# First weight sum of gate/up tiles 1 to 4 by two DMAs, and rewritten issue orders, in a fused SSD + latent-attention + SwiGLU layer

## The chip, the cores and the metric

The kernel runs on one core of one Trainium2 chip. The metric is device time in microseconds of one execution; several executions are timed and their median is given. The engines of the core are TensorE (PE; the loading of its stationary operand is listed apart, as PEld), VectorE (DVE), ScalarE (ACT), GpSimd (POOL) and SyncE (SP), which here only issues DMAs. Each engine carries out its own list of instructions in order; between engines semaphores order the work.

## The reference

One layer of a hybrid encoder for 512 prompt and 64 sample tokens (576 columns in all), width 1024, followed by a final norm. Everything is float32.

```
h = rmsnorm(x);  z, xbc, dt, cq, ckv, kr = split(h @ w_in)
y_ssd = rmsnorm(ssd_scan(silu(conv(xbc)), dt, ...) * silu(z))       # chunked state space heads
o     = mla_attend(q(cq), keys(ckv, kr)) @ w_uv                     # latent attention, block-causal
x = x + concat(y_ssd, o) @ w_out
hf = rmsnorm(x)
x = x + (silu(hf @ w_gate) * (hf @ w_up)) @ w_down                  # D_FF = 2816
y = rmsnorm(x)
```

The change touches the weights of `hf @ w_gate` and `hf @ w_up`.

## The kernel before

All activations lie transposed, features on the 128 partitions and tokens along the free axis; 576 tokens are two halves of 288. Float32 accuracy is reached by three products of fp32r operands: every weight and activation is split into a high part (a cast on ScalarE, L127) and a low part (a subtraction on VectorE, L128).

**Stages.** In-projection (0 to about 35 us), convolution and state sums, the SSD scan, attention, out-projection (to about 255 us), gate/up and down (to about 600 us), final norm. In the feed-forward part D_FF is cut into 22 tiles of 128 columns; tile f has one step for gate and up (`gu_steps`, tile 0 in `gu_first`), and after every four tiles a down step (`down_steps`), part of whose results is added into `x2` by accumulating DMAs from GpSimd's queue (L1047).

**Seven products in place of eight.** Gate and up of one tile and the two halves of the tokens form a 2x2 block product, calculated by the Strassen/Winograd scheme: `block_product` (L894) multiplies one of A11, A12, S4, A22, S1, S2, S3 with one of seven sums of activation blocks. The weight sums S1 to S4 are made on the chip, in `block_weights`:

- `r2` and `r1`, 128 x 1024 floats each (512 KB), are loaded on SP's queue (L847, L848). One half of each holds one block of the 2x2.
- L850: left half of `s1` = left of `r2` + right of `r2`. This is S1.
- L851: left half of `s2` = left of `r2` - left of `r1` (S3).
- L852: right half of `s1` = S1 - left of `r1` (S2).
- L853: right half of `s2` = right of `r1` - S2 (S4).
- Then A22, A11/A12, S1/S2 and S3/S4 are split: casts on ScalarE (L855, L127), subtractions on VectorE (L861, L128).

In the trace `gu` stands for all of `r2`, `r1`, `s1`, `s2` (named gu{f}_0, _1, _2, _3 in this order), `wh_gu_S`, `wl_gu_S`, `wh_gu_A`, `wl_gu_A` and `gu_a` for their split forms. The down weights (`db`) go through the same function.

**Slots.** The buffers of the four raw tensors come from a pool of 8 slots of 4 KB per partition, and a table (`PLACES`) says which buffer gets which slot. Around the change: slot 0 holds an out-projection weight, then gu1_2, gu3_2 and a down weight; slot 2 an out-projection weight, gu2_2, gu4_2, gu5_2; slot 4 gu1_0, gu2_0, gu4_1; slot 1 gu1_1, gu2_1, gu4_0, gu5_0; slots 3 and 5 hold out-projection weights and then gu3_0 and gu3_1; slot 6 gu2_3 and gu4_3; slot 7 gu1_3 and gu3_3. A load into a slot waits until the last reader of the buffer before it is done.

**Order.** The engines don't issue in the order of the program. At the end of the file `issue_in_order` (L1274) takes, for each of the five engines, a list in `ISSUE` that names the engine's instructions by their number of creation, and ties each to its predecessor in that list. So the place of an instruction in a list fixes which instructions of its engine stand ahead of it; it starts when these have been issued and its operands are there. The steps of each stage are created in the order of `ORDER_CONV`, `ORDER_SSD`, `ORDER_ATT` and `ORDER_FFN`.

Of the kernel before, what the change touches and what calls it, by code (L numbers as in the profile page):

```python
# [37 lines left out]
BLOCKS = tuple(range(0, LAST - 1, 4))  # L38
SEEDED = (4, 5, 6, 7)
# [17 lines left out]
def hybrid_layer_kernel(ctx: ExitStack, tc: tile.TileContext, a, o):  # L57
# [783 lines left out]
    def block_weights(src1, src2, name, blocks):  # L841

        n = len(gu_dma)
        sums = dve
# [5 lines left out]
        sums.tensor_tensor(l(s1), l(r2), r(r2), ALU.add)  # L850
# [423 lines left out]
def issue_in_order(tc, nc):  # L1274
# [45 lines left out]
602-612 637 641-644 638-640 657-659 665-688 660 689-736 661-662 737-760 771-794 663-664 645-652 763-766 653-656  # L1320
795-818 767-770 761-762 819-826 859-861 833-836 862-864 827-832 865-866 837-839 867 880-883 840 868-870 841 845-852
871-873 853-856 874-879 842-843 904-906 857-858 884-887 907-909 844 888 910-912 892-903 889-891 913-915 925-934
916-921 935 939-940 922-924 936-938 949-957 964-965 941 966 945-948 967-969 942-944 970-971 958-963 972-974 976-979
975 987-988 980 984-985 1003 991-993 981-983 986 1015 1004-1006 989 994-995 1016-1021 996 1007-1014 1022-1026
1029-1034 997 1043-1045 990 1000-1002 998-999 1046-1054 1035-1042 1027-1028 1059-1060 1055 1075-1092 1056-1058
1093-1104 1121-1123 1065-1067 1124 1061-1062 1071-1072 1063-1064 1130-1132 1068-1070 1125-1129 1073 1133-1156
1105-1108 1074 1229-1237 1119-1120 1238 1241 1239-1240 1242-1252 1157 1111-1114 1109-1110 1253-1264 1158 1176
1265-1276 1115-1118 1159-1161 1177-1179 1162-1175 1277-1285 1289-1290 1180-1183 1188-1189 1184-1187 1205-1206
1190-1192 1227 1193-1198 1291-1297 1199-1201 1228 1202-1204 1286-1288 1215-1220 1207-1214 1221 1318 1222-1224 1298
1225-1226 1299-1306 1319 1307 1320 1308-1317 1321-1322 1330-1332 1323 1342-1343 1348-1351 1344-1345 1352-1354 1346  # L1330
1355 1347 1333 1324-1329 1334-1341 1356-1363 1368 1364-1366 1369-1370 1367 1371-1393 1404 1394-1396 1405-1406
1397-1403 1407-1415 1428 1416-1427 1429-1433 1440-1441 1434-1435 1442 1436-1439 1572 1443-1447 1452 1448 1453-1456
1449 1457-1458 1450 1459-1460 1451 1461-1462 1587 1578 1584 1463 1581 1573 1464-1478 1579 1479-1486 1575 1488 1487
1489 1585 1490-1497 1500 1498 1501-1503 1499 1586 1588 1504-1506 1576 1574 1507 1580 1508-1509 1512 1577 1513 1510
1514-1515 1511 1516-1517 1605 1518-1522 1593 1523-1525 1582-1583 1526-1527 1606 1528-1531 1602 1536 1532 1537 1533
1538 1534 1603 1539 1607 1535 1589 1540-1541 1599 1542-1544 1594 1608 1545-1550 1600 1551-1552 1595 1614 1553-1555
1609 1560 1556-1557 1626 1561-1565 1615 1558-1559 1566-1568 1616 1569-1570 1604 1571 1596 1590 1597-1598 1601 1591
1610 1617 1620 1623 1621 1635 1627 1622 1592 1636 1629 1637 1628 1611 1641 1618 1630 1624 1631 1612-1613 1625
1658-1659 1642 1644 1650 1660 1647 1661-1662 1632-1633 1663 1651 1648 1664-1665 1619 1656 1638-1640 1666 1643 1667
1634 1668 1645 1669 1646 1649 1652-1654 1657 1694 1670-1672 1695-1697 1673 1682 1698 1655 1674 1699 1675 1700 1718  # L1340
1683 1719 1676-1677 1701 1678 1684 1702 1679 1685 1703 1680 1704 1686 1681 1720 1687 1721 1688 1722-1723 1689 1724
1690-1691 1706 1692-1693 1725 1707 1726 1705 1727-1728 1708-1709 1730 1710-1711 1729 1712 1731-1732 1713-1717
1733-1734 1778-1779 1735 1780 1754 1736 1755 1742 1756 1743-1744 1781 1737 1782 1745-1746 1766 1747-1749 1767 1783
1750-1752 1738 1768 1753 1757-1758 1769 1739-1740 1759 1741 1770 1784 1760 1785-1786 1771 1787 1761-1762 1802 1788
1803 1772 1789 1763 1773 1804-1805 1774 1806-1813 1764-1765 1775-1776 1838 1777 1839-1841 1862-1864 1842 1865
1843-1846 1866 1790 1867 1814 1847 1791 1848 1868 1792 1849 1869 1793 1870-1872 1794-1795 1873 1815-1818 1874-1875
1819 1796 1820 1797 1876 1798-1799 1877 1800 1878-1880 1850-1851 1881 1801 1821 1882 1822 1883 1823 1884 1852-1853
1826 1885 1827 1824 1828 1825 1829 1854 1830-1831 1855 1832 1856 1886-1887 1833 1857-1860 1888 1834 1889-1890 1861
1891 1835 1892 1836 1893 1837 1894-1900 1910-1913 1901-1903 1922 1946 1923 1904 1914-1915 1905-1907 1947 1924 1948
1916-1917 1934-1937 1925 1918-1919 1949 1920 1938 1926-1927 1939-1940 1921 1950 1928 1908 1929 1909 1951 1930 1952  # L1350
2024 1941 1970 1931 2025 1971 1932-1933 1942-1944 1953 1972 1945 1954-1956 1958-1959 1973 1960 1974-1975 1961 1976
1962-1963 1977 1964 2026 1965-1966 2027-2028 1967 1978 1957 2029 1968-1969 2000 1979 2012 1980-1982 2054 1983
1988-1989 2042 2013 1990 2043 2055 2006 2056 2014-2015 1991 2007 2001 2044 2048 1992-1993 2057 2002 2058-2059 1984
2008-2009 2045 2016 2003-2005 1985-1986 2017 2049 2046-2047 1994 1987 1995 2010 1996 2011 2018 1997 2060-2061 2019
2062 2020-2021 2030 2063 2022 2031 2064 2023 2065-2066 2050 2067-2069 1998 2032 2070 2051-2052 1999 2053 2033
2071-2073 2034 2074-2075 2084-2086 2076 2078 2035 2077 2079 2036 2087 2080-2081 2037 2088 2082 2114 2083 2102 2090
2089 2038 2091 2103 2039-2040 2115 2092 2041 2093 2104 2094 2105 2095 2106 2096 2107 2116-2118 2138 2097-2099 2139
2108 2100 2109 2101 2119 2110 2192 2111-2112 2120 2113 2121 2126 2122 2127 2123 2128-2130 2140 2131 2144 2132 2145
2193 2133 2124 2134 2146-2148 2135 2149-2150 2136 2194 2137 2141 2125 2142 2195-2196 2151 2143 2197 2156 2152-2153
2157-2158 2154 2159 2168 2160-2162 2180 2155 2163 2181 2169 2164-2165 2182 2174 2222 2170-2171 2216 2166 2210 2175  # L1360
2172 2183 2173 2167 2184 2223 2217 2176 2211 2177 2224 2186 2212 2225 2187-2188 2218 2178-2179 2219 2213-2215 2185
2189-2190 2226 2191 2234 2198 2220 2199-2200 2235 2228-2230 2221 2204 2231-2232 2236 2201 2237-2239 2233 2227
2205-2206 2240 2202 2246 2241 2203 2242 2252 2243-2245 2207 2247 2253-2254 2248 2270 2255 2208 2282 2256-2258 2283
2259-2260 2271-2272 2261 2284 2262-2264 2273 2285 2209 2265 2286 2266 2274 2267 2275 2268 2287 2269 2288-2289 2276
2290 2277 2249 2306 2291-2292 2294 2278 2295 2307 2279 2296 2280-2281 2297-2303 2293 2318-2319 2308 2304 2309-2310
2320 2305 2311 2250 2321-2323 2312-2313 2251 2314 2330 2315-2316 2331 2317 2332-2333 2324 2334-2335 2325-2326 2336
2354 2327 2366-2367 2337 2342 2338 2368-2370 2343 2339-2340 2371 2355 2328 2344-2348 2356 2349 2372 2341 2350-2352
2357 2373-2374 2358 2353 2390 2375 2359-2361 2376 2362-2363 2329 2364-2365 2377-2382 2391-2393 2402-2403 2394
2404-2405 2383-2385 2395 2386 2406 2387 2407 2388-2389 2408 2396-2398 2409 2399-2400 2410 2401 2414-2418 2438 2411
2419-2420 2426-2428 2421 2429 2422 2450 2412 2423-2424 2451 2439 2430-2431 2413 2452 2440 2432 2425 2453 2441-2442  # L1370
2433 2443-2444 2434 2445 2435 2446 2436 2447 2437 2454 2528 2474 2448 2529 2455-2457 2530 2449 2531-2532 2475-2476
2462 2477 2533 2458-2459 2463-2464 2478-2479 2465-2466 2480 2558 2467 2481 2468-2471 2482 2472-2473 2483 2516 2559
2484-2485 2460 2486 2461 2487 2492 2517 2493 2560 2518 2546 2504 2494 2488 2519 2552 2495-2497 2553 2505 2520 2547
2506-2507 2521 2548 2498-2499 2549 2489 2500 2510 2501 2508 2502 2550-2551 2561 2490 2509 2554 2503 2511 2491 2555
2512-2513 2562-2563 2514-2515 2570 2522-2523 2571 2524 2556 2525 2564 2526-2527 2557 2534-2535 2565 2572 2566-2569
2540 2582-2584 2573 2541 2574 2542 2585 2575-2576 2536-2539 2588 2577 2589 2586 2578-2579 2590 2543 2580-2581
2591-2592 2606-2609 2544 2610 2594-2595 2545 2593 2587 2596-2597 2611-2613 2598 2618 2599-2601 2619 2614 2602
# [123 lines left out]
685 682 681 688-690 679 692 687 693-700 691 701-704 683 705-719  # L1501
# [111 lines left out]
```

## Time and profile before

| | |
|---|---|
| Median of 3 runs | 640.44 us (639.99 to 640.5) |
| Profiled execution, its own time | 639.58 us |
| Profiled execution, span | 637.5 us |
| Granted TensorE clock | 0.998 |
| Weights of gate/up | 44 loads of 512 KB, one L850 add for each of 22 tiles |
| GpSimd | 111 instructions, none between 192 and 304 us |

The span reaches from the first to the last instruction of the profile; the run's time has 2.1 us more around it. In the rows that follow, a line number belongs to the kernel above, `out<-in` are the names of the program with buffer numbers left out, and `xN` counts instructions. TensorE's matmuls are pipelined: one of 288 columns shows a duration of about 0.29 us, while the next one starts 0.13 us after it, so durations overlap and starts count.

### The profile page before, as it was taken

Reading aid. Unit: us, or ns where it says so; the run is one execution under the profiler, and the core shown is the slowest. Engines: PE = TensorE matmul, PEld = TensorE weight load, DVE = VectorE, ACT = ScalarE, POOL = GpSimd, SP = SyncE. Lnnn points to the kernel's source line nnn. Section 1 sums busy time; section 2 is a strip of 40 time slices with the busy share of each in tenths; the row PEclk is TensorE's granted clock in tenths of the full one; section 3 lists DMA queues with packets and bytes.
Section 4 is the critical chain, followed back from the end, with each engine's and each line's share of the span. In section 5 each row is a group of like instructions: output and inputs, shape, how many; then the busy total and the mean of one; then the engine's idle time right before and its main releaser. Section 6 shows DMA issues by size and latency. Waiting matters only on the chain.

```text
span 637.5 us, 11950 instructions
## 1 busy us (share of the span) xinstructions
PE 626.2 (98%) x4639; PEld 598.0 (94%) x4639; DVE 551.4 (86%) x980; ACT 390.4 (61%) x751; POOL 70.7 (11%) x111
## 2 busy tenths in 40 slices
PE   9999999999999999999999999999999999999994
PEld 9899999985887899999999999999999999999994
DVE  6999996899867599999998997889888998998763
ACT  7655425789766479955656565655565656545463
POOL 1322122001010000000012002100211011100022
PEclk9999999999999999999999999999999999999999
DMA  9522185314131132231187427550765274723004
GB/s 310 207 51 78 35 209 151 114 30 147 72 111 34 62 131 73 93 108 67 36 202 158 128 91 163 141 136 40 189 159 133 67 182 111 181 74 133 1 1 149
DMA packets 31560, 72.66 MB, mean 114 GB/s; under 512 B 3706, under 2 KB 11400, under 8 KB 31248
## 3 DMA queue, kind: packets, MB, share of 16 engines
q1 hardware_dynamic: 25360, 60.77, 29.8%
q0 software_dynamic: 5424, 10.57, 9.3%
q8 instruction: 36, 0.59, 0.4%
q10 hardware_dynamic: 720, 0.57, 0.3%
q14 instruction: 20, 0.16, 0.1%
HBM read 58.03 MB, written 3.30 MB: 96 GB/s over the span
## 4 chain that ended last, share of the span: by engine, by line
PE 48%; issue 1%; DVE 1%; ACT 1%; POOL 1%; POOLq 0%; DVEq 0%
PE ps_x L894 17%; PE ps_dx L1034 9%; PE ps_z L894 9%; PE ps_dz L1034 5%; PE ps_y L894 4%; PE ps_dy L1034 2%; PE ps_l L1104 2%; POOL x L1157 0%; DVE x L1145 0%; DVE sq_last L1194 0%; DVE ss L1192 0%; POOL ss L1238 0%; POOLq L1600 0%; ACT sq L1233 0%; ACT x L1149 0%
## 5 line engine op out<-in xcount | busy, mean ns | idle before, releaser
L894 PE MATMUL ps_x<-xop,wh_gu_S 128*128 128x288 f32 x504 | 126.2, 295 | 0.0
L894 PEld LDWEIGHTS ps_x<-xop,wh_gu_S 128*128 128x128 f32 x504 | 88.2, 188 | 0.7 <-ACT u L963 0.2
L894 PE MATMUL ps_x<-xop,wl_gu_S 128*128 128x288 f32 x252 | 73.2, 295 | 0.0
L894 PE MATMUL ps_z<-xop,gu_a 128*128 128x288 f32 x252 | 61.7, 295 | 0.0
L127 ACT CAST wh_gu_S<-gu 128x1024 fp32r<-128x1024 f32 x44 | 46.2, 1053 | 14.8 <-PE ps_y L894 4.2
L128 DVE TENSOR_TENSOR wl_gu_S<-gu,wh_gu_S 128x1024 fp32r<-128x1024 f32 x44 | 52.8, 1217 | 0.8 <-ACT wh_gu_S L127 0.5
L894 PEld LDWEIGHTS ps_x<-xop,wl_gu_S 128*128 128x128 f32 x252 | 47.1, 188 | 0.0
L1047 POOL DMA_DIRECT2D x<-db x16 | 14.9, 930 | 277.9 <-ACT db L1040 247.8
L143 PE MATMUL ps_in<-xs,wh_in 128*128 128x288 f32 x256 | 45.5, 298 | 0.0
L894 PE MATMUL ps_y<-xop,wh_gu_A 128*128 128x288 f32 x168 | 44.9, 295 | 0.0
L894 PEld LDWEIGHTS ps_z<-xop,gu_a 128*128 128x128 f32 x252 | 43.5, 188 | 0.0
L894 PE MATMUL ps_z<-xop,wh_gu_S 128*128 128x288 f32 x168 | 43.4, 295 | 0.0
L894 PE MATMUL ps_x<-xop,wh_gu_A 128*128 128x288 f32 x168 | 42.7, 295 | 0.0
L143 PEld LDWEIGHTS ps_in<-xs,wh_in 128*128 128x128 f32 x256 | 37.8, 189 | 0.2
L127 ACT CAST wh_gu_A<-gu 128x1024 fp32r<-128x1024 f32 x22 | 23.1, 1051 | 23.0 <-PE ps_x L894 16.1
L894 PEld LDWEIGHTS ps_y<-xop,wh_gu_A 128*128 128x128 f32 x168 | 30.1, 188 | 0.1
L894 PEld LDWEIGHTS ps_z<-xop,wh_gu_S 128*128 128x128 f32 x168 | 29.7, 188 | 0.0
L128 DVE TENSOR_TENSOR wl_gu_A<-gu,wh_gu_A 128x1024 fp32r<-128x1024 f32 x22 | 26.8, 1217 | 3.3 <-ACT wh_gu_A L127 1.8
L894 PEld LDWEIGHTS ps_x<-xop,wh_gu_A 128*128 128x128 f32 x168 | 29.5, 188 | 0.0
L465 PE MATMUL ps_o<-cat_y,wh_out 128*128 128x288 f32 x128 | 29.0, 312 | 0.0
L143 PE MATMUL ps_in<-xs,wl_in 128*128 128x288 f32 x128 | 27.5, 296 | 0.0
L465 PE MATMUL ps_o<-cat_o,wh_out 128*128 128x288 f32 x128 | 27.3, 297 | 0.0
(594 smaller groups left out, 2002.8 us busy)
## 6 DMA issues: line engine op xcount, KB each, us to landing
gu<-in_w_gu SPq DMA_DIRECT2D x44, 512.0 KB, 4.8
db<-in_w_down SPq DMA_DIRECT2D x16, 512.0 KB, 4.5
x<-db POOLq DMA_DIRECT2D x16, 288.0 KB, 6.5
x<-dc POOLq DMA_DIRECT2D x16, 288.0 KB, 4.1
wr_in<-in_w_in SPq DMA_DIRECT2D x8, 512.0 KB, 6.2
wr_out<-in_w_out SPq DMA_DIRECT2D x8, 512.0 KB, 3.3
cumb<-cumD SPq DMA_DIRECT2D x5, 512.0 KB, 5.0
x<-in_xT SPq DMA_DIRECT2D x2, 1152.0 KB, 6.6
```

The costliest lines, as they stand in the source:

```text
L127: act.copy(hi, raw)
L128: dve.tensor_tensor(lo, raw, hi.bitcast(F32), ALU.subtract)
L143: pe.matmul(ps[:m, hf, :n], w, x[:, hf * n : (hf + 1) * n], start=start and k == 0 and i == 0, stop=stop and k == last and i == 2,)
L465: pe.matmul(ps[:, :n], w, x[:, cols], start=not onto and k == 0 and i == 0, stop=onto or (k == len(terms) - 1 and i == 2), skip_group_chec ...
L894: pe.matmul(ps, p, q, start=not onto and first and kp == kps[0] and j == 0, stop=onto or (last and kp == kps[-1] and j == 2), skip_group_c ...
L1034: pe.matmul(ps, l, r, start=not onto and k == 0 and j == 0, stop=onto or (k == n - 1 and j == 2), skip_group_check=onto,)
L1047: pool.dma_start(x2[t], v, accum_op=ALU.add)
L1104: pe.matmul(ps, w, x[:, cols], start=first and k == 0 and i == 0, stop=last and k == len(terms) - 1 and i == 2,)
```

## The change

For the four tiles named, S1 is no longer an add on VectorE. A second load brings the left half of the same source once more, straight into the left half of `s1` (128 x 512 floats, 256 KB, SP's queue); then GpSimd's queue issues an accumulating DMA that adds the right half of the source to it (256 KB). Everything that follows from S1 stays as it was. The second DMA waits for the first, both wait for the slot of `s1`, and L852 and the split of S1 wait for the second.

The lists of `ISSUE` are rewritten: the first place that differs is 630 of TensorE's (about 94 us in the trace of before), 156 of VectorE's (about 96 us), 78 of ScalarE's (about 93 us), 74 of GpSimd's and 40 of SP's. Up to there nothing differs. TensorE and ScalarE keep the number of their instructions; VectorE's list is four shorter, SP's and GpSimd's four longer each. `PLACES` is unchanged.

```
+SUMS_BY_DMA = ('gu1', 'gu2', 'gu3', 'gu4')
...
         sp.dma_start(shaped(r2), src2)
         gu_dma.append(sp.dma_start(shaped(r1), src1).ins)
         l, r = ((lambda z, i=i: (blocks if z is r1 or z is r2 else halves_of)(z)[i]) for i in range(2))
-        sums.tensor_tensor(l(s1), l(r2), r(r2), ALU.add)
+        if name in SUMS_BY_DMA:
+            sp.dma_start(s1[:, :512], src2[:, :512])
+            pool.dma_start(s1[:, :512], src2[:, 512:], accum_op=ALU.add)
+        else:
+            sums.tensor_tensor(l(s1), l(r2), r(r2), ALU.add)
         sums.tensor_tensor(l(s2), l(r2), l(r1), ALU.subtract)
         sums.tensor_tensor(r(s1), l(s1), l(r1), ALU.subtract)
         sums.tensor_tensor(r(s2), r(r1), r(s1), ALU.subtract)
...
     "POOL": """
-0-3 7 18 28 4 8 5 9 6 10 26-27 11 29 12-17 20-22 19 23-25 31 30 32-42 53 55 57 59 54 56 58 60 43-52 61-73 75 74 76-77
-79 78 80-85 87 86 88-89 91 90 92-93 95 94 96-111
+0-3 7 18 28 4 8 5 9 6 10 26-27 11 29 12-17 20-22 19 23-25 31 30 32-42 53 55 57 59 54 56 58 60 43-52 61-77 79 78 80-81
+83 82 84-89 91 90 92-93 95 94 96-97 99 98 100-115
 """,
     "SP": """
-11-14 16 15 18 17 19-20 22 21 25 24 39 23 37 26 40 33 38 41-43 34 44 32 45 81 46-48 57 64 79 59 58 56 62 61 65 63 60
-83 70 74 67 69 68 71 78 80 88 73 75 72 66 89 77 76 82 86 90-92 87 93 100 103 101-102 104-105 109-118 120 119 122-123
...
+11-14 16 15 18 17 19-20 22 21 25 24 39 23 37 26 40 33 38 41-43 34 44 32 45 81 46-48 57 64 79 59 58 56 62 61 60 65 63
+83 70 68-69 74 67 78 71 80 75 66 73 72 88 77 76 89 82 91 86 90 87 92-93 100 103 101-102 104-105 109-111 114-115 112
+116 113 117-118 120 119 121-122 124 123 126 125 128 127 130 129 131-132 134 133 135-140 142 141 144 143 145-146 148
...
```

Read out, SP's list around these tiles is, before and after ("S1" is the new load):

| before | after |
|---|---|
| gu1_0, gu1_1 | gu1_0, gu1_1 |
| gu2_0, gu2_1 | S1 of gu1, S1 of gu2 |
| gu3_0, gu3_1 | gu3_0, gu2_0, gu3_1, gu2_1 |
| gu4_0, gu4_1 | S1 of gu3, gu4_0, S1 of gu4, gu4_1 |
| db0_0_0, db0_0_1 | db0_0_0, db0_0_1 |

GpSimd's four new DMAs stand behind the last of its attention work (about 178 us) and ahead of the first accumulating DMA of the down step (about 319 us). Places of some instructions in VectorE's list, counted from 0: L852 of tile 1 was 414 and is 418; the subtraction of tile 1's S1/S2 (L128) was 445 and is 441; L852 of tile 2 was 430 and is 445; L852 of tile 3 was 468 and is 460; L852 of tile 4 was 483 and is 475. In TensorE's list changes between a matmul of plain fp32 operands and one of fp32r operands number 108 before and 192 after.

More of the change, by code (lines that the diff above doesn't have):

```diff
@@ L1324 @@
[L1324 to L1333, printed above, removed]
@@ new lines @@
+1749-1751 1737 1752 1784-1785 1767 1756 1786 1768 1753 1787 1769 1757 1738 1770 1739 1802 1758 1740 1771 1741
+1759-1760 1772 1788 1803-1805 1789 1806-1807 1761 1808-1813 1762 1773-1774 1763-1764 1775 1765 1776 1838-1839 1777
+1862 1840 1863-1864 1841-1842 1790 1865 1843-1846 1866 1847-1848 1867 1849 1791 1868 1792 1814 1869-1872 1874 1793
+1875 1794 1873 1815 1795-1796 1816 1797 1817-1818 1798 1850 1799-1800 1819-1820 1876 1801 1821 1877-1878 1851
+1879-1882 1822 1883 1852 1823 1826 1853-1854 1824 1884 1827-1828 1885 1825 1829-1830 1855-1857 1831 1886 1832
@@ new lines @@
+4190 4162 4206 4169 4191 4163 4192 4226 4170 4227 4238 4164 4171 4165 4193 4198 4172 4199-4200 4173 4201 4174 4239
+4175-4177 4194 4184 4240 4202 4207 4228-4229 4241 4230 4208-4209 4231 4195 4185 4242 4210 4243 4186 4232 4211-4212
+4262 4213 4263 4233-4234 4223 4214 4244 4217 4203 4235 4264 4236 4245 4204 4218 4220 4215-4216 4224 4265 4225 4221
+4266 4219 4267 4246 4237 4268 4250-4252 4247 4253 4274-4275 4254 4276-4277 4248 4222 4278 4269-4272 4249 4279 4273
+4255-4259 4280 4260-4261 4281-4391
@@ L1477 @@
+890 918 912 866 914 920-921 898 924 891 923 925 933 892 922 928 927 926 935 934 936 930 929 931-932 937-938 942 940
+939 943 947 941 945 944 950 946 948-949 951-975
 """,
@@ new lines @@
+563 566 564 569 568 567 571 570 561 572 565 577 574 578 575 573 580 582 576 579 589 586 581 588 587 583 592 590 597
+584-585 591 594 602-603 595 599 596 600 605 601 598 604 606 611 593 609 608 610 612-613 630 614 607 619 624 616 625
+615 617 621 618 622 626 623 620 627-628 633 631 636-637 629 634-635 632 640 638-639 643 645 644 648 646 651 654 649
+641 647 656 655 650 657 659 658 663 660-661 642 664-666 652 674 667 675 669 653 662 670 668 676-677 671 673 672 678
+680 686 684 682 688 690 692-699 687 700 689 701 681 683 679 685 702-704 691 705-719
```

331 lines of the change are left out of this document (166 added, 165 removed).

## The prediction

> **What bounds the kernel now.** First the page's totals and the chain of work that ended last:
>
> ```profile
> span 637.5 us, 11950 instructions
> PE 626.2 (98%) x4639; PEld 598.0 (94%) x4639; DVE 551.4 (86%) x980; ACT 390.4 (61%) x751; POOL 70.7 (11%) x111
> PE 48%; issue 1%; DVE 1%; ACT 1%; POOL 1%; POOLq 0%; DVEq 0%
> ```
>
> TensorE sets the end: it is busy for all but 11.3 us of the span, and the named part of the chain is nearly all TensorE. An edit pays only where it takes a hole out of TensorE's stream, and costs only where it makes one. So I read next the busy time by stretches, around the edited sums and where the order lists begin to differ (columns: busy us of PE, PEld, DVE, ACT, POOL with instruction counts, granted clock, DMA share, GB/s).
>
> ```profile
> 80.00:224.00 144.00, 142.74 (x1041) 121.76 (x1040) 113.18 (x248) 93.51 (x244) 14.40 (x25) 1.00 0.34 105
> 144.00:160.00 16.00, 14.75 (x76) 9.54 (x76) 15.77 (x41) 15.23 (x44) 1.96 (x4) 1.00 0.45 146
> 224.00:336.00 112.00, 111.90 (x831) 110.37 (x830) 110.88 (x185) 79.04 (x134) 3.38 (x4) 1.00 0.33 101
> 240.00:256.00 16.00, 16.00 (x122) 15.92 (x121) 15.79 (x30) 15.43 (x32) 0.00 (x0) 1.00 0.20 67
> 256.00:272.00 16.00, 16.00 (x117) 15.54 (x116) 15.97 (x31) 14.23 (x25) 0.00 (x0) 1.00 0.32 104
> 288.00:304.00 16.00, 16.00 (x122) 15.92 (x122) 15.26 (x25) 8.99 (x14) 0.00 (x0) 1.00 0.20 67
> ```
>
> VectorE is full from 224 to 336 us (110.88 of 112), yet TensorE has no hole there (111.90 of 112). VectorE sits just under the limit and not on it. At 144 to 160 us TensorE does run dry for 1.25 us, and that stage lies inside the rewritten part of the order lists. In the gate/up stage a better order could only shorten the pitch of the matmuls: 831 starts at 16/122 = 0.131 us are 109.0 us of the 112, so 3.0 us at most, and some of that is slower kinds of matmul (the norm sums among them).
>
> **What is removed.** Four adds at L850, of tiles 1 to 4. Their group, and three neighbours from VectorE's timeline (start, duration, line):
>
> ```profile
> L850 DVE TENSOR_TENSOR gu<-gu x22: 678/681/694, 222.8 to 573.2; 128x512 f32<-128x512 f32 x22
> 286.49 0.68 DVE L853 TENSOR_TENSOR gu<-gu,gu 128x512 f32<-128x512 f32 x1
> 287.09 0.68 DVE L850 TENSOR_TENSOR db<-db 128x512 f32<-128x512 f32 x1
> 287.69 0.45 DVE L971 TENSOR_TENSOR g<-ps_y,R 128x288 f32<-128x288 f32 x1
> ```
>
> One add lasts 0.68 us, but the next instruction starts 0.60 us after it (287.09 to 287.69), so four give back 4 x 0.60 = 2.4 us of VectorE. Does TensorE see it? The first of this time comes free before 262 us, and there ScalarE stands in the way:
>
> ```profile
> 260.57 1.05 ACT L127 CAST wh_gu_S<-gu 128x1024 fp32r<-128x1024 f32 x1
> ```
> ```profile
> 239.52 0.68 DVE L850 TENSOR_TENSOR gu<-gu 128x512 f32<-128x512 f32 x1
> 249.04 0.46 DVE L820 TENSOR_TENSOR xv<-xv 128x288 f32<-128x288 f32 x1
> 262.09 1.21 DVE L128 TENSOR_TENSOR wl_gu_S<-gu,wh_gu_S 128x1024 fp32r<-128x1024 f32 x1
> 264.32 0.44 DVE L914 TENSOR_TENSOR u<-u,ps_p 128x288 f32<-128x288 f32 x1
> ```
>
> The subtraction for tile 1's S1/S2 (262.09) needs the cast that ends at 260.57 + 1.05 = 261.62. By count of the new list, VectorE would reach it at 262.09 - 2.4 = 259.7: two adds are gone (1.2), and two operations of tile 2 ahead of it have moved behind it (1.2). ScalarE's list up to that cast ends as before and ScalarE is 15.43 of 16 busy at 240 to 256 us, so I don't expect an earlier cast. VectorE then idles about 1.9 us and the gain there is spent. The value for the removal is -0.4 us, between 0 (TensorE has no hole to fill) and -2.4 (every freed microsecond reaches it).
>
> **What is added.** Per tile a 256 KB load on SP's queue and a 256 KB accumulating one on GpSimd's. No row shows these; the nearest are the two accumulating groups' statistics (288 KB; issue ns, then issue to landing), and a plain 256 KB load:
>
> ```profile
> L1047 POOL DMA_DIRECT2D x<-db x16: 862/862/1205, 318.8 to 543.1; - x16
> DMA to landing us min/median/max: 3.4/4.8/8.2
> wr_uqr<-in_w_uqr SPq DMA_DIRECT2D x1, 256.0 KB, 2.6
> ```
>
> So a sum is ready 2.6 + 0.86 + 4.8 = 8.3 us after its slot is free, between 6.9 and 11.7. GpSimd has nothing else to do between 192 and 304 us, so its waits delay nobody. [...]
>
> Tile 1: the slot is free by 239.52 (the old add writes it then), so the sum is there at 247.8 (246.4 to 251.2). Its first reader, L852, is at place 418 of the new list: all that before had done by 249.04 except the add, L852 and L853, so 249.04 - 1.8 = 247.2. Stall 0.6 (0 to 4.0); the idle 1.9 us at S1/S2 covers the middle value. Tile 3's slot is free once tile 1's S1/S2 is subtracted, 261.6 + 1.1 = 262.7, plus 8.3 = 271.0 (269.6 to 274.4). Its reader stands, in operations of 0.37, 0.60 and 1.14 us pace, some 10 us behind that subtraction, at about 272.9: no stall at the middle, 1.5 at the upper end. Tiles 2 and 4 have likewise about 9.6 us between freeing and reading. I take 0 for all four, 0 to 4.0 as bounds.
>
> **What is moved past a queue.** SP's queue issues in order, and the new list puts tile 2's loads behind tile 3's first. SP's rows of before, and a burst of four 512 KB loads to price the new one:
>
> ```profile
> 243.62 0.33 SPq L847 DMA_DIRECT2D gu<-in_w_gu  x1
> 246.33 0.33 SPq L848 DMA_DIRECT2D gu<-in_w_gu  x1
> 255.41 0.33 SPq L847 DMA_DIRECT2D gu<-in_w_gu  x1
> 255.84 0.38 SPq L848 DMA_DIRECT2D gu<-in_w_gu  x1
> ```
> ```profile
> L134 SPq DMA_DIRECT2D wr_dl<-in_w_dlast x4: 328/376/426, 577.3 to 579.2; - x4
> DMA to landing us min/median/max: 3.5/5.2/7.4
> ```
>
> Tile 3's first load waits at 255.41 for a slot that an out-projection weight holds. Tile 2's pair, at 243.62 and 246.33 in before, now follows it: about 255.8 and 256.6, the second being the last of four. It lands 3.5 to 7.4 us later, 260.1 to 264.0; I take 264.0, as it is the last of its burst like the 7.4 row. VectorE's first reader of it, L852 of tile 2, moved from 253.44 to place 445: 264.32 less four operations of 0.60 (two adds, and L851 and L852 of this tile) is 261.9, or 261.62 + 1.14 + 3 x 0.37 = 263.9 with the ScalarE wait above. Stall 0.1 (0 to 2.1). Measured against before's pace, VectorE must start it by 264.32 - 1.2 = 263.1 to lose nothing; it is 0.9 us late, and the two adds still to vanish (tiles 3, 4) give 1.2 back. ScalarE's cast of tile 2's A11 stands at about 266 us, behind the landing. Cost on TensorE: 0 (0 to 0.9).
>
> **The rewritten order.** From about 93 us on all lists differ, though the work is the same. TensorE changes between fp32 and fp32r matmuls 192 times instead of 108, counted in the lists. Its timeline prices a change:
>
> ```profile
> 165.25 0.29 PE L465 MATMUL ps_q<-cqn,wl_pair 128*128 128x288 f32 x1
> 165.39 0.27 PE L702 MATMUL ptp<-ident,pr 128*128 128x128 f32 x1
> 165.41 0.62 PE L465 MATMUL ps_k<-ckv,wh_pair 128*128 128x416 f32 x2
> 165.88 0.35 PE L465 MATMUL ps_k<-ckv,wl_pair 128*128 128x416 f32 x1
> 166.06 0.59 PE L680 MATMUL sc<-ks,qs 100*128 100x256 f32 x2
> 166.50 0.71 PE L702 MATMUL ptp<-ident,pr 128*128 128x128 f32 x5
> 166.96 0.62 PE L465 MATMUL ps_k<-ckv,wh_pair 128*128 128x416 f32 x2
> 167.42 0.35 PE L465 MATMUL ps_k<-ckv,wl_pair 128*128 128x416 f32 x1
> ```
>
> A 416-column fp32r matmul takes 166.06 - 165.88 = 0.18 to 0.19. One transposition alone: 165.88 - 165.25 = 0.63, less 0.13 and 2 x 0.19, is 0.12. Five in a row: 167.42 - 166.50 = 0.92, less 0.38, over five is 0.108. So a pair of changes costs about 0.012 us, and 42 more pairs 0.5 us (0 to 0.5 for this kind; the kinds that use half the columns may be dearer). I take +0.5. The order's effect on waits I can't see ahead: TensorE's idle 1.26 us between 80 and 224 us (144.00 less 142.74) could vanish or double, -1.3 to +1.3, value 0.
>
> **Sum.** 639.58 (profiled run: span 637.5 and 2.1 around it) - 0.4 + 0 + 0 + 0.5 + 0 = 639.7. The median of the runs stands 0.86 us above the profiled run, so the forecast is 640.5, written 640.6: no change, within the 0.2% (1.28 us) that a measurement of this kernel can tell.
>
> **Rivals.**
> *Freed VectorE time reaches TensorE, and the new order closes the attention stage's hole.* For it: VectorE 110.88 of 112, so every list in that stage hangs on it, and 117 starts in 256 to 272 us against 122 nearby (5 x 0.131 = 0.7 us). Against it: TensorE's 111.90 of 112, and ScalarE's cast. Price: 0.7 + half of the 1.26 us hole + half of the other adds' 1.2 = 1.9 us, so 638.5.
>
> *Tile 2's second load decides (the other side).* One mechanism: SP's queue at 255.4 us. If it lands after 263.1, VectorE, full until 336 us, passes the delay on: to the release of the PSUM banks behind it (L914), to R2, to the low halves that TensorE's tile 1 and 2 products read. For it: four 512 KB loads in a burst, and a moved issue 10 us later. At 264.0 it costs 0.9; with tile 3's sum at its upper end as well delayed by the same shift, and tile 4's behind it, up to 0.9 + 1.5 + 1.5 = 3.9. Middle 2.4: 642.9. Against it: TensorE's products of tile 2 begin only at 266.7 us, and other tiles' products can run between. [...]
>
> *The new order starves TensorE in the attention stage.* For it: 144 to 160 us, where VectorE is 15.77 and ScalarE 15.23 of 16: transpositions, their copies and the products that read them are placed closer there in the new lists. Against it: elsewhere in 80 to 224 us VectorE is 113.18 of 144. Price: the 1.26 us hole once more, and half again, 1.9 us: with the switches 642.4.
>
> *The sums aren't taken from the path because the path never was there* (the change does what it says and it is worth nothing) is the forecast itself.
>
> **How the numbers follow.** Forecast 0.32 (own range 639.2 to 641.8), first rival 0.30, second 0.24, third 0.14. Faster than 639.16: 0.30 and 0.03 of the forecast = 0.33. Slower than 641.72: 0.38 and 0.04 = 0.42. Same: 0.25. The range: downwards the first rival with all of the hole and the full 0.7 and 1.2, 640.5 - 3.2 = 637.3; upwards tile 2's case with 3.9, 644.4.
>
> **What would show it.** Right: L850 x18 in its group; the TensorE window 256 to 272 us still 16.00 with about 117 starts; VectorE idle before the S1/S2 subtraction, released by ScalarE, near 262 us; tile 2's loads on SP at about 255.8 and 256.6; the waits of L852 on a DMA under 1 us in all. Wrong, to the fast side: 80 to 224 us shorter by over 1 us, or over 119 starts in 256 to 272. Wrong, to the slow side: L852 waiting for a DMA by over 2 us and a named TensorE wait on VectorE behind it, or new waits on L702 and L727 between 140 and 224 us.

## The result, and the profile after

| | before | after |
|---|---|---|
| Median of 6 runs each | 640.47 us (639.78 to 640.84) | 647.7 us (644.76 to 649.72) |
| Profiled execution: its time, span, granted clock | 639.58, 637.5, 0.998 | 644.76, 643.1, 0.993 |

The changed kernel is slower: 1.0111 times the time before, 95% interval 1.0077 to 1.0145, or 7.2 us. The forecast was 640.6, the range ended at 644.4. Its six runs lie in two groups, 644.76, 645.48 and 645.87 us (clock 0.990 to 0.993) and 649.54, 649.64 and 649.72 us (0.985 to 0.988), and the profiled one is of the first group, so its trace explains 5.2 us (644.76 less 639.58). A second trace of the same kernel, further down, shows what a longer run has more.

The page after: totals, and the chain of work that ended last.

```profile
span 643.1 us, 11977 instructions
PE 628.0 (98%) x4639; PEld 600.1 (93%) x4639; DVE 553.2 (86%) x976; ACT 390.7 (61%) x751; POOL 74.2 (12%) x115
PE 74%; DVE 11%; DMA 6%; issue 5%; ACT 3%; POOL 1%; POOLq 0%; SPq 0%; DVEq 0%; ACTq 0%
```

VectorE, ScalarE and DMA now stand in a chain whose named part had been TensorE's almost alone. Busy time by stretches, columns as in the prediction:

```profile
80.00:224.00 144.00, 140.84 (x1024) 120.09 (x1024) 114.95 (x246) 93.65 (x243) 13.60 (x25) 1.00 0.33 100
96.00:112.00 16.00, 15.31 (x119) 15.09 (x118) 11.05 (x17) 8.31 (x23) 2.59 (x3) 1.00 0.49 141
144.00:160.00 16.00, 14.14 (x73) 9.65 (x72) 15.32 (x39) 14.06 (x40) 1.96 (x4) 1.00 0.25 87
224.00:336.00 112.00, 112.00 (x839) 111.30 (x838) 109.81 (x181) 77.61 (x134) 7.01 (x8) 1.00 0.43 125
336.00:600.00 264.00, 262.96 (x1979) 262.03 (x1978) 234.15 (x373) 154.32 (x262) 24.22 (x28) 1.00 0.48 125
```

And before, the two stretches that the prediction did not show:

```profile
96.00:112.00 16.00, 16.00 (x124) 16.00 (x124) 10.82 (x18) 9.36 (x26) 3.24 (x4) 1.00 0.51 148
336.00:600.00 264.00, 264.00 (x1992) 263.74 (x1991) 235.88 (x374) 153.70 (x260) 24.37 (x29) 1.00 0.48 125
```

Read the starts of TensorE, at 0.131 us each; in microseconds this is an estimate, since not all matmuls are of one size. From 80 to 224 us 17 are missing (1024 for 1041, 2.2 us), of which 96 to 112 us, the state sums, has 5. The stretch with the edited sums has 8 more than before (839 for 831, a gain of 1.0 us), and the feed-forward behind it 13 fewer (1.7 us). So the stage of the edit gained, and the loss is where the order changed and the edit is not. Whether the edit or its stage's order gained, this trace doesn't tell; a pair of kernels further down does. From 600 us on, two matmuls of the final part give fixed points:

```profile
624.46 0.28 PE L1104 MATMUL ps_l<-pr,wl_dl 128*128 128x256 f32 x1
627.19 1.83 PE L1251 MATMUL ps_warm_last<-ones 128*128 128x128 f32 x14
629.03 1.16 PE L1257 MATMUL ps_r<-Rp,ident 128*128 128x128 f32 x8
```
```profile
626.78 0.28 PE L1109 MATMUL ps_l<-pr,wl_dl 128*128 128x256 f32 x1
630.74 3.15 PE L1256 MATMUL ps_warm_last<-ones 128*128 128x128 f32 x14
633.68 1.40 PE L1262 MATMUL ps_r<-Rp,ident 128*128 128x128 f32 x8
```

First fence before, second after (line numbers are 5 higher there: L857 is the old L852). The last product of the down step (`ps_l`) starts 626.78 - 624.46 = 2.32 us late; from it to the last broadcast of the norm (`ps_r`) it is 6.90 us where it was 4.57, another 2.33; and from `ps_r` to the end of the span 9.42 for 8.47, 0.95. That is the whole 5.6 us of span. The fourteen matmuls on ones into `ps_warm_last` are the same work in both: 1.83 us at a granted clock of 1.00 and 3.15 us at a mean of 0.54.

**Who waits in the state sums.** ScalarE, VectorE and GpSimd around 95 us, before:

```profile
93.17 0.69 ACT L410 ACTIVATE cth<-cacc 128x579 f32<-128x579 f32 x1 [5.67 <-DVE cacc L408]
94.79 0.21 DVE L413 SCALAR_TENSOR_TENSOR bc<-cth,cacc 128x64 f32<-128x64 f32 x1
96.07 0.68 POOL L523 TENSOR_SCALAR_AFFINE_SELECT cumb<-cumb 64x512 f32<-64x512 f32 x1
```

After:

```profile
94.76 0.67 ACT L411 ACTIVATE cth<-cacc 128x579 f32<-128x579 f32 x1
95.46 0.23 DVE L414 SCALAR_TENSOR_TENSOR bc<-cth,cacc 128x64 f32<-128x64 f32 x1 [0.89 <-ACT cth L411]
95.97 2.08 DVE L413 SCALAR_TENSOR_TENSOR bc<-cth,cacc 128x512 f32<-128x512 f32 x1
95.77 1.72 POOL L524 TENSOR_SCALAR_AFFINE_SELECT cumb<-cumb 64x512 f32<-64x512 f32 x2
```

The new ScalarE list puts other work ahead of the last tanh of the convolution, so it comes 1.6 us later (94.76 for 93.17). The 512-column part of VectorE's product of that tanh (`bc`) then falls together with GpSimd's selects and lasts 2.08 us. Before, the 64-column part was over at 95.00, ahead of the select. TensorE loses 0.69 us at 96 to 112 us (15.31 of 16.00) by this. More of the idle time lies in the attention stage: from 136 to 168 us TensorE's holes are 0.12, 0.20, 1.66 and 0.40 us by stretches of 8 us, 2.38 us in all, where before had 1.25. The waits named there are for ScalarE and VectorE, ahead of the scores (0.44 and 0.48 us) and of the transpositions (0.74, which were 0.92 and 0.21 before).

### The profile page after: what moved, and what is told of

It reads as the page before. It is cut to its first block, busy times and chain, and to the rows that moved or that the text cites. A ratio compares the mean times of both kernels' runs of the same rounds, so it can differ in the third digit from the quotient of the medians.

```text
span 643.1 us, 11977 instructions
## 1 busy us (share of the span) xinstructions
PE 628.0 (98%) x4639; PEld 600.1 (93%) x4639; DVE 553.2 (86%) x976; ACT 390.7 (61%) x751; POOL 74.2 (12%) x115
## 4 chain that ended last, share of the span: by engine, by line
PE 74%; DVE 11%; DMA 6%; issue 5%; ACT 3%; POOL 1%; POOLq 0%; SPq 0%; DVEq 0%; ACTq 0%
PE ps_x L899 16%; PE ps_z L899 8%; PE ps_o L466 8%; PE ps_in L144 7%; PE ps_dx L1039 6%; PE ps_y L899 4%; PE ps_dz L1039 3%; PE ps_z L466 3%; PE ps_first L144 2%; DMA x<-db 2%; PE ps_l L1109 2%; PE sc L681 2%; PE ps_p L899 2%; PE ps_dy L1039 2%; PE pv L728 1%
## 5 line engine op out<-in xcount | busy, mean ns | idle before, releaser
L899 PE MATMUL ps_x<-xop,wh_gu_S 128*128 128x288 f32 x504 | 123.8, 295 | 0.3
L128 ACT CAST wh_gu_S<-gu 128x1024 fp32r<-128x1024 f32 x44 | 46.1, 1052 | 10.8 <-PE ps_x L899 4.3
L899 PE MATMUL ps_y<-xop,wh_gu_A 128*128 128x288 f32 x168 | 46.2, 295 | 0.0
L899 PE MATMUL ps_x<-xop,wh_gu_A 128*128 128x288 f32 x168 | 44.0, 295 | 0.0
L128 ACT CAST wh_gu_A<-gu 128x1024 fp32r<-128x1024 f32 x22 | 23.1, 1051 | 23.0 <-PE ps_x L899 11.6
L466 PE MATMUL ps_o<-cat_y,wh_out 128*128 128x288 f32 x128 | 31.8, 325 | 0.4 <-DVE cat_y L160 0.4
L466 PE MATMUL ps_z<-xs,wh_z 128*128 128x288 f32 x128 | 26.7, 304 | 0.7 <-DVE zh L477 0.7
```

What stands on the lines that cost most here:

```text
L128: act.copy(hi, raw)
L466: pe.matmul(ps[:, :n], w, x[:, cols], start=not onto and k == 0 and i == 0, stop=onto or (k == len(terms) - 1 and i == 2), skip_group_chec ...
L899: pe.matmul(ps, p, q, start=not onto and first and kp == kps[0] and j == 0, stop=onto or (last and kp == kps[-1] and j == 2), skip_group_c ...
```

## The experiments

Each kernel was timed beside the kernel before on the same chip; a figure with a sign is the median less before's median of the same session (640.41, 639.93, 640.32 and 640.45 us in the four sessions). A letter for a theory in an expectation is a working name; the text beside it says which cause was on trial.

**Which part of the lists costs the time.** The two sets of lists were joined at times of the trace, the instructions of each side in that side's order. Three kernels leave the sums on VectorE; the fourth has the added DMAs, with the new lists in that stage alone.

```
+SUMS_BY_DMA = ()                               # mid_lists_dma: ('gu1', 'gu2', 'gu3', 'gu4')
 ISSUE = the new order from .. to ..            # and before's elsewhere
   early_lists: start-222 us   mid_lists_dma: 222-336   ffn_lists: 336-600   end_lists: 597-end
```

> The new lists up to 222 us (state sums, scan, attention), the old ones behind, all four sums on VectorE. Theory A (the new lists cost, stretch by stretch; in the trace of the changed kernel TensorE is 2.0 us behind at 222 us): +1.5 to +2.3 us over before, new named waits of TensorE between 93 and 112 us (zh, ptp, qs). Theory B (the sums by DMA cost, the lists are neutral): within 0.5 us of before. Theory C (half of the runs near 649.6 us because TensorE's clock drops in the attention stage after a longer hole): two groups of runs about 4 to 5 us apart here; if the drop is at the end of the program, one group.

> The old lists up to 222 us, the new ones from there to 336 us with the four sums by DMA, the old ones behind. Theory A: -1.0 to +0.5 us against before (TensorE's lag fell from 2.0 us at 222 us to about 1.2 us at 334 us in the changed kernel). Theory B: +4 us or more, with VectorE waiting at L857 for a DMA by over 2 us and TensorE behind it.

> The new lists from 336 to 600 us alone, sums on VectorE. Theory A: +1.0 to +1.8 us (the lag grows from 1.2 us at 334 us to 2.5 us at 600 us, with one TensorE wait on wl_gu_A near 340 us and one near 486 us). Theory B: within 0.5 us of before.

> The new lists from 597 us on alone (last down tiles and final norm), sums on VectorE. Theory A: +2.0 to +3.0 us, of which 1.3 us because the granted clock is 0.5 while the last matmuls run. Theory B: within 0.5 us of before. Theory C: if the drop that makes two groups lies in the end part, some runs 4 to 5 us above the others here; if it lies in the attention stage, one group.

| | median of n | ratio, 95% | less before |
|---|---|---|---|
| early_lists | 643.69 of 12 | 1.0052 (1.0031 to 1.0072) | +3.3 |
| mid_lists_dma | 639.69 of 10 | 0.9990 (0.9975 to 1.0005) | -0.7 |
| ffn_lists | 641.48 of 10 | 1.0011 (0.9997 to 1.0024) | +1.1 |
| end_lists | 641.78 of 12 | 1.0022 (1.0009 to 1.0035) | +1.4 |

The DMAs and the order around them cost nothing; the early part costs most. The four add up to 5.0 of 7.2 us; the intervals of mid_lists_dma and ffn_lists include no change. The early part costs more than was expected (1.5 to 2.3), the end less (2.0 to 3.0), and the twelve runs of early_lists, 640.52 to 647.51 us, show no two groups. The trace of early_lists shows the state sums with nothing else changed. ScalarE, VectorE, GpSimd and TensorE:

```profile
93.23 0.63 ACT L531 ACTIVATE ecp<-ecp 128x512 f32<-128x512 f32 x1 [1.28 <-DMA ecp<-cumD]
...
94.93 0.67 ACT L411 ACTIVATE cth<-cacc 128x579 f32<-128x579 f32 x1
95.63 1.74 DVE L414 SCALAR_TENSOR_TENSOR bc<-cth,cacc 128x64 f32<-128x64 f32 x1 [1.25 <-ACT cth L411]
95.56 1.72 POOL L524 TENSOR_SCALAR_AFFINE_SELECT cumb<-cumb 64x512 f32<-64x512 f32 x2
97.43 0.47 PE L516 MATMUL ps_b<-bc 128*64 128x64 f32 x2 [1.97 <-DVE bc L414]
```

The exponential of `ecp` waits 1.28 us for a DMA, and the cast, the two `el` and the tanh queue behind it. Then `bc`, 64 columns, takes 1.74 us for 0.21, and ends at 95.63 + 1.74 = 97.37, 0.09 us behind the selects' end of 95.56 + 1.72 = 97.28; TensorE stands dry for 1.97 us. In the trace of old_end (an experiment further down) the 512-column `bc` starts at 95.47, 0.11 us ahead of the selects, and lasts 2.38 us all the same; behind the selects, at 97.66 us in early_lists, it lasts 0.68. So a start ahead of the selects did not keep it short, and why it lasts longer beside them no run shows. What the hole does next, in windows of 1 us of early_lists:

```profile
96.00:97.00 1.00, 0.00 (x0) 0.00 (x0) 1.00 (x1) 0.35 (x1) 1.00 (x2) 1.00 0.74 217
97.00:98.00 1.00, 0.57 (x3) 0.46 (x4) 1.00 (x3) 0.06 (x1) 0.28 (x1) 0.56 1.07 351
98.00:99.00 1.00, 1.00 (x7) 0.93 (x6) 0.62 (x2) 0.30 (x1) 0.00 (x0) 0.50 1.14 157
99.00:100.00 1.00, 1.00 (x6) 1.00 (x5) 1.00 (x3) 0.20 (x1) 0.00 (x0) 0.50 0.29 49
```

In the window in which TensorE gets its operand (97.43), its granted clock falls to 0.50. A mean of 0.56 in one window is 0.88 us at half clock, two windows follow whole, and 0.74 in the window from 100 us is 0.52 more (1.00 in the next): about 3.4 us in all, which by estimate (half of 3.4) is 1.7 us of TensorE's work. Ahead of it stood 1.97 us without work. Not every hole is followed by a low clock: sums_on_vector and the second trace of the changed kernel have the same hole (1.97 and 1.96 us) and a low clock behind it (means of 0.67 and 0.90, and of 0.91 and 0.66, in the two windows of 4 us from 96 us), but end_filled, an experiment further down, has the hole and keeps the clock:

```profile
97.37 0.33 PE L516 MATMUL ps_b<-bc 128*64 128x64 f32 x2 [1.97 <-DVE bc L414]
98.00:99.00 1.00, 1.00 (x11) 1.00 (x10) 1.00 (x3) 0.10 (x1) 0.00 (x0) 1.00 1.13 153
```

What decides between the two, no run here shows. In the first trace of the changed kernel the hole was only 0.69 us, and the clock stayed at 1.00.

**One order of ScalarE, one stage, one edit at a time.** Against the changed kernel, run again beside them:

```
 tanh_first, ScalarE's list (75: the last tanh of the convolution, L411)
-... 92 73-74 89 104 94 79 90 75 84 80 78 ...
+... 92 73-74 89 75 104 94 79 90 84 80 78 ...
 sums_on_vector
-SUMS_BY_DMA = ('gu1', 'gu2', 'gu3', 'gu4')
+SUMS_BY_DMA = ()          # the four sums right ahead of each tile's L857 in VectorE's list
 old_end: before's lists from 600 us on, all engines
 both_mended: tanh_first and old_end together
```

> The changed kernel once more, beside the three that follow. Theory A+gate (holes that the new lists make at 95 to 99 us and in the end part cost 2 to 3 us each, and in a share of the runs TensorE's clock halves for some us behind them): +5 to +9 us over before, spread over more than 3 us from run to run, the slower runs with the lower mean clock. Theory B (sums by DMA): the same median, but without a spread that goes with the clock.

> The changed kernel with one instruction of ScalarE's list moved four places forward: the last convolution tile's tanh (L411) stands ahead of the second exponential (L531), the cast of wh_z1 and the two el. Theory D (that tanh is late, so VectorE's bc is late and meets GpSimd's selects, and TensorE runs dry at 95 to 99 us): 2 to 4 us below the changed kernel, no TensorE wait on bc or zh near 96 us, bc products 0.2 and 0.7 us long in place of up to 2.1, and most of the spread gone. Rival (the loss of that stage lies in the order of TensorE's own list): within 0.7 us of the changed kernel.

> The changed kernel's lists with the four sums back on VectorE, each right ahead of its L857, and no added DMA. Theory A (the lists cost, the DMA sums do not): within 1 us of the changed kernel, a little slower rather than faster, as VectorE has 2.4 us more to do. Theory B (the DMA sums cost): back within 1 us of before.

> The changed kernel up to 600 us, the old lists behind. Theory A: 1.4 to 3 us below the changed kernel, the granted clock 1.00 until the last matmul in most runs. If the spread of the changed kernel comes from the end part, it goes; if from the hole at 96 us, it stays.

> The changed kernel with both repairs: the tanh four places forward, and the old lists from 600 us on. Theory A+D: the two stretches account for the loss, so 640 to 642 us, within 2 us of before, the rest of it at 340, 408 and 486 us. Rival (a loss spread over all the lists): 643 us or more.

| | median of n | ratio, 95% | less changed_again |
|---|---|---|---|
| changed_again | 647.6 of 5 | 1.0114 (1.0098 to 1.0130) | |
| tanh_first | 643.13 of 10 | 1.0056 (1.0036 to 1.0076) | -4.5 |
| sums_on_vector | 649.78 of 4 | 1.0144 (1.0127 to 1.0161) | +2.2 |
| old_end | 644.1 of 6 | 1.0071 (1.0052 to 1.0091) | -3.5 |
| both_mended (next session) | 641.93 of 12 | 1.0023 (1.0010 to 1.0037) | -5.7 |

Moving one instruction in ScalarE's list is worth 4.5 us, a little more than expected. The trace of tanh_first shows the tanh early again and `bc` short on both its parts, ahead of the selects, and TensorE has no hole at 96 to 112 us (16.00 of 16.00, 126 starts, clock 1.00):

```profile
92.72 0.69 ACT L411 ACTIVATE cth<-cacc 128x579 f32<-128x579 f32 x1
94.34 0.22 DVE L414 SCALAR_TENSOR_TENSOR bc<-cth,cacc 128x64 f32<-128x64 f32 x1
94.84 0.68 DVE L413 SCALAR_TENSOR_TENSOR bc<-cth,cacc 128x512 f32<-128x512 f32 x1
95.95 1.70 POOL L524 TENSOR_SCALAR_AFFINE_SELECT cumb<-cumb 64x512 f32<-64x512 f32 x2 [0.34 <-ACT el L499]
```

Most of the spread was expected to go with this, and it did not: the ten runs lie between 640.96 and 647.01 us, and the traced one is the slowest. That trace has another hole, 1.75 us at 408 us (its cause is shown below), with a clock of 0.84 and 0.73 in the two windows of 4 us from 408 us. The holes of the attention stage are there as well (6.34 us busy of 8 at 152 to 160 us, as in the changed kernel).

Taking the DMA sums away makes it slower still, by 2.2 us in four runs where at most 1 us was expected: the sums help. Against before, sums_on_vector prices the new order without the DMA sums: 649.78 for 639.93 us, some 9 us. The two mends together give 5.7, less than 4.5 + 3.5.

The profiled run of changed_again has a span of 647.1 us, 4.0 more than the first trace of the same kernel. Its windows of 4 us up to 600 us where the clock differs from that trace:

```profile
96.00:100.00 4.00, 2.06 (x15) 2.00 (x16) 3.42 (x6) 1.42 (x4) 1.79 (x3) 0.91 0.95 214
...
160.00:164.00 4.00, 3.27 (x10) 2.01 (x10) 3.59 (x10) 3.65 (x10) 0.47 (x1) 0.59 1.05 367
```

The window left out, 100 to 104 us, has a clock of 0.66. In the other run all three have 1.00, and 27, 32 and 23 starts for 15, 23 and 10. So two more stretches at half clock set the 647.1 us apart from the 643.1, and with them a hole at 96 to 100 us that is longer by 1.25 us (2.06 us busy for 3.31). The longer hole begins with a DMA: the exponential of `ecp` starts at 94.18 for 93.06 us, so the tanh starts at 95.88 for 94.76, and the 64-column `bc`, which had slipped in ahead of the selects at 95.46, now starts at 96.58, behind them, and lasts 1.30 us. The second stretch, at 160 to 164 us, follows holes of 0.44, 0.48 and 0.73 us; the first trace has the same three (0.44, 0.48 and 0.74) and keeps 1.00. The trace of changed_again also shows a hole at 408 us. VectorE:

```profile
408.69 0.69 DVE L855 TENSOR_TENSOR gu<-gu 128x512 f32<-128x512 f32 x1 [2.62 <-DMA gu<-in_w_gu]
```

and TensorE:

```profile
412.26 0.40 PE L899 MATMUL ps_x<-xop,wl_gu_A 128*128 128x288 f32 x1 [1.66 <-DVE wl_gu_A L129]
```

The new VectorE list has a sum of tile 11 ahead of tile 10's low half; it waits 2.62 us for its load, and TensorE 1.66 us for what stands behind it. The first trace has no wait of TensorE there.

**The sums by themselves, and the last hole.**

```
 mid_dma_again: mid_lists_dma once more
 mid_vector: the same lists, SUMS_BY_DMA = (), the four sums right ahead of each tile's L857
 sum11_later: both_mended, and in VectorE's list (671, 673: L855 and L857 of tile 11)
-... 654 647 671 673 655 646 656 672 ...
+... 654 647 655 646 656 671 673 672 ...
```

> The old lists except from 222 to 336 us, with the four sums by DMA, once more beside the same with sums on VectorE. Expected from the first run: 0 to 1.3 us below before. If the DMA sums are worth something, they show against the next kernel, by 0.5 to 2.2 us.

> The same lists as the kernel ahead of it, with the four sums on VectorE, each right ahead of its L857. Theory A: up to 2.2 us slower than with the DMA sums (VectorE is full there and these lists leave no room for four adds). Theory B: faster than with the DMA sums.

> The kernel with both repairs, and in VectorE's list the two sums of tile 11 (L855, L857) moved behind the subtraction wl_gu_A of tile 10. Theory F (VectorE waits for tile 11's late load while TensorE waits for wl_gu_A): no TensorE wait on wl_gu_A near 410 us, and 0.8 to 1.8 us below the kernel with two repairs, 640 to 641 us. Rival (the load itself is what TensorE lacks a little later): the hole moves by some us and the time stays.

mid_dma_again took 639.15 us of 12 (0.9986, 0.9976 to 0.9997), mid_vector 641.27 of 12 (1.0022, 1.0012 to 1.0032): with the lists of that stage otherwise alike the DMAs are worth 2.1 us. Only this one place for the four sums in those lists was tried; against before, whose lists give the sums places of their own, the DMAs and their lists together gain 1.2 us (639.15 for 640.32). Windows of the two, in this order:

```profile
224.00:336.00 112.00, 112.00 (x843) 111.72 (x843) 110.14 (x182) 80.24 (x139) 6.99 (x8) 1.00 0.43 121
```
```profile
224.00:336.00 112.00, 111.36 (x821) 109.17 (x821) 110.52 (x181) 77.64 (x133) 3.52 (x4) 1.00 0.33 101
```

VectorE is as full in both (110.14 and 110.52), but TensorE starts 22 matmuls more with the DMAs. mid_dma_again is thus quicker than the kernel before, and the best of this study; the same kernel as mid_lists_dma was 0.7 us quicker, within its interval. sum11_later took 640.9 of 11 (1.0009, 0.9997 to 1.0021), 1.0 less than both_mended's 641.93, but of another session, and the intervals of the two overlap. What the edit did is shown by the traces, both_mended first, 400 to 416 us:

```profile
400.00:416.00 16.00, 14.57 (x110) 14.33 (x109) 13.57 (x23) 9.41 (x18) 2.61 (x3) 1.00 0.62 149
```
```profile
400.00:416.00 16.00, 16.00 (x123) 16.00 (x122) 14.90 (x24) 9.68 (x19) 2.60 (x3) 1.00 0.68 166
```

both_mended has a hole of 1.43 us there, sum11_later none; that it is worth 1.0 us is likely and not shown.

**The end.** ScalarE's new list makes five gains (L1154) in a row ahead of squares (L1238) that TensorE's norm sums wait for. In the changed kernel:

```profile
623.86 2.31 ACT L1154 ACTIVATE x<-x,par 128x320 f32<-128x320 f32 x5
```
```profile
627.00:631.00 4.00, 2.43 (x23) 1.25 (x23) 1.61 (x4) 3.36 (x10) 2.00 (x3) 1.00 0.51 175
631.00:634.00 3.00, 3.00 (x16) 3.00 (x16) 0.88 (x3) 0.75 (x3) 0.00 (x0) 0.50 0.27 94
```

TensorE is 2.43 of 4 us busy, and then gets 0.50 of its clock; the fourteen matmuls took 3.15 us in that time. Two causes are thus possible for the end's cost: the order of ScalarE, or the clock. Two kernels fill the holes with matmuls on ones, one restores ScalarE's list, and end_again is end_lists once more, as their base.

```
 end_filled (on the changed kernel: n = 3), end_one_fill (on end_lists: n = 1)
+        fill(n)                                 # pe.matmul(warm[:, :P], ones, ones), n times
         packed(pn1, ss3[:, parts[1]], True, False)
         for t in range(NP, KT):
+            if t > NP:
+                fill(n)
             packed(pn1, q[t], False, t == KT - 1)
 end_old_scalar (on end_lists), ScalarE's list
-... 677 676 671 673 672 678 680 686 684 682 688 ...
+... 677 676 671-672 686 673 684 680 678 685 682 ...
```

> The changed kernel with 12 more matmuls of ones into the bank that keeps TensorE warm, three in each hole between the last norm sums, results not used. Theory (the granted clock of 0.5 while the last matmuls run costs 1.4 us or more, and it drops because TensorE is only 0.6 busy for 4 us): the clock stays 1.00 until the last matmul, 14 records of warm-up matmuls take 1.8 us in place of 3.2, and the time is 1 to 2 us below the changed kernel's. Rival (the drop has nothing to do with the holes): no gain, or up to 0.5 us lost.

> The new lists from 597 us on alone, once more, as the base of the next two. From the first run: 0.6 to 2.3 us over before.

> The same, with ScalarE's list as in before also from 597 us on, so that the gains of the first column part (L1154) stand ahead of the squares TensorE waits for, and TensorE's, VectorE's and GpSimd's lists new. Theory E (the end part's loss is the squares behind five gains): back to within 0.5 us of before, no clock of 0.5 before the last matmul. Rival (the order of TensorE's last down products, or the clock by itself): still 1 us or more over before.

> The new end lists with one matmul of ones in each of four holes between the norm sums in place of three. Theory (clock): full clock to the last matmul and 0.7 to 1.5 us below the base, as one fits into a hole of 0.41 us. Rival (a hole of 0.41 us filled once is still too thin): the base's time and a clock of 0.5.

end_filled took 647.04 us of 6 (1.0107, 1.0074 to 1.0140); end_again 641.56 of 11 (1.0015, 1.0003 to 1.0026), end_old_scalar 641.6 of 11 (1.0020, 1.0005 to 1.0034), end_one_fill 641.4 of 12 (1.0020, 1.0010 to 1.0031). None of the three edits moved the time beyond its interval: end_filled is to be set against the changed kernel (647.6 and 647.7 us), the other two against end_again. None gave the gain that its theory expected; the trace of end_one_fill has the full clock to its last matmul, but so has that of its base. In end_filled the clock did hold:

```profile
626.56 0.28 PE L1109 MATMUL ps_l<-pr,wl_dl 128*128 128x256 f32 x1
631.73 1.83 PE L1250 MATMUL ps_warm_last<-ones 128*128 128x128 f32 x14
633.57 1.16 PE L1269 MATMUL ps_r<-Rp,ident 128*128 128x128 f32 x8
```

The fourteen took 1.83 us again, but from `ps_l` to `ps_r` it is 7.01 us, as long as the 6.90 without the filling: the norm sum waits for the squares, and the twelve matmuls put between stand ahead of it in TensorE's list. In end_old_scalar the tail was repaired and the time was not:

```profile
627.05 0.28 PE L1109 MATMUL ps_l<-pr,wl_dl 128*128 128x256 f32 x1
631.61 1.16 PE L1262 MATMUL ps_r<-Rp,ident 128*128 128x128 f32 x8
619.34 0.81 PE L1231 MATMUL ps_n<-ss,ones 128*128 128x320 f32 x2 [0.82 <-DVE ss L1197]
```

4.56 us from `ps_l` to `ps_r`, before's 4.57, where end_again has 5.80 (630.30 less 624.50) in its trace at full clock. So 1.24 us of the tail are ScalarE's order. The trace of end_lists, the same program, has the clock of 0.50 there, fourteen matmuls in 3.15 us, and 7.20 us from `ps_l` to `ps_r` (632.53 less 625.33): by this difference the low clock cost that run 1.40 us. The 6.90 us of the changed kernel have both in them. But a new wait of 0.82 us stands at 619 us, on a VectorE sum: ScalarE's old order does not fit the other engines' new ones. What each engine's list costs of the end's 1.1 to 1.4 us stays open, and so does why the end's lists cost 3.5 us within the changed kernel (old_end) and less than half of it alone.

## Why the prediction was wrong, point by point

- **The step that failed**: "The order's effect on waits I can't see ahead: TensorE's idle 1.26 us between 80 and 224 us (144.00 less 142.74) could vanish or double, -1.3 to +1.3, value 0." The new order measured some 9 us without the DMA sums (sums_on_vector) and 7.2 us with them. The term was mis-sized in three ways. The idle time in that stretch rose to 3.16 us, by 1.9. The bound covered 80 to 224 us alone, though "From about 93 us on all lists differ": 336 to 600 us and the end were given no term, and inside the stretch only the hole at 144 to 160 us was looked at, not the state sums at 96 us, where the new order makes one that before doesn't have. And it counted a hole at its own length, while a hole here can have two further prices: a late VectorE instruction that met GpSimd's selects lasted 1.1 to 1.7 us longer (1.30 and 1.74 us for 0.21, 2.08 and 2.38 for 0.68), and about 3.4 us at half clock followed in three traces.
- **The rival nearest in mechanism** was "The new order starves TensorE in the attention stage" (0.14, 642.4). Its 1.9 us is the idle time that 80 to 224 us gained in the profiled run, and the attention stage, taken as 136 to 168 us, holds 1.13 of it; its own window, 144 to 160 us, holds 0.61 (14.75 to 14.14). It had one cause right, then, though the new waits there stand ahead of the scores and not of the transpositions. It didn't have the first and dearest hole, behind the tanh at 93 us: moving that one instruction gave -4.5 us, with the holes of the attention stage left as they were.
- **The removal, -0.4 (0 to -2.4).** Removal and DMAs together measured -2.1 with the lists of the change (mid_dma_again against mid_vector) and -0.7 and -1.2 against the kernel before. All lie within the bounds, on the first rival's side of the value: its gain in that stage was there, then, and the argument that ScalarE's cast eats it did not hold. The cast did end late, at 260.95 + 1.06 = 262.01 us, but VectorE, whose order had changed, had other work till then; the subtraction started at 262.64 with no wait named ahead of it.
- **What is added, 0, was right.** The group of accumulating DMAs and their statistics:

```profile
L853 POOL DMA_DIRECT2D gu<-in_w_gu x4: 856/878/936, 243.6 to 277.7; - x4
DMA to landing us min/median/max: 4.2/4.2/4.7
```

  4.2 us where 4.8 was taken from the 288 KB ones. The plain loads of S1 took 2.9 to 3.4 us, where 2.6 was taken, so load, issue and landing add up to 3.0 + 0.88 + 4.2 = 8.1 us by their medians, forecast 8.3. L857, the old L852, waited for a DMA twice, 0.20 us at tile 0, which has no such sum, and 0.35 us for a load of tile 2.
- **Moved past a queue, 0, was right.** Tile 2's loads were issued at 256.9 and 257.8, forecast 255.8 and 256.6 (tile 3's first load, ahead of them, stood at 256.40 for 255.41 before, so the trace was already 1.0 us late there). The second landed after 7.4 us, the figure that the forecast took, and tile 2's L857, at 265.31, waited 0.35 us for it; TensorE had 117 starts and no hole from 256 to 272 us, as forecast. The second rival (tile 2's load decides, 642.9) has its sign right and its cause wrong.

- **The changes of operand type, +0.5,** were not measured alone. The stretch from 224 to 336 us gained starts, so they were no loss there that outweighs the rest. The sum itself, 639.7 + 0.86, gives 640.5; the 640.6 that was written decides nothing.
- **Of the sum** 7.2 us: the early lists 3.3, the middle -0.7, the feed-forward 1.1, the end 1.4, together 5.0. The remaining 2.2 us belong to no part alone and stay open; the changed kernel itself came out alike twice (647.7 and 647.6 us). That the holes bring the low clock is read from their order in time and from tanh_first, where the hole at 97 us and the low clock behind it went together; it is argued and not shown, as equal holes were followed by both clocks. At the end it stays open in the same way: end_filled, with its holes filled, and end_again, with them, both kept the full clock in their traces, and end_lists, the same program as end_again, did not.

## What to carry to other kernels

When an edit comes with a rewritten order, price the order first: compare the lists stage by stage and look, in each, for an instruction that waits for a DMA and now stands ahead of one that TensorE needs. Find the cause by joining old and new orders at a few points in time; that told here that the edit was worth having and its order was not. Keep the edit and the order of its own stage, and leave the rest as it was: that version (639.15 us) beat both kernels.

## What the runs showed of the hardware that was not expected

- A 64-column VectorE instruction grew from 0.21 to 1.74 us, and a 512-column one from 0.68 to 2.08, when they met two affine selects of GpSimd (early_lists and the changed kernel). Moving them by 1.1 to 1.3 us took this away (0.22 and 0.68 us in tanh_first).
- A dry TensorE of 2.0 us was followed by a granted clock of 0.50 for about 3.4 us in three traces (early_lists, sums_on_vector, changed_again) and by the full clock in a fourth (end_filled). At 627 to 631 us, 2.43 us of work in 4 were followed by it in the changed kernel, while end_again with like holes kept 1.00. The same 14 matmuls took 1.83 us and 3.15.
- The two traces of the changed kernel lie 4.0 us apart: the longer has two stretches at half clock that the shorter lacks, one behind a longer hole and one behind holes of the same length.
